# Gate and up products by seven block products for eight, and the down projection in three parts

## The chip, the cores and the metric

One core of a Trainium2 chip runs the whole program. The metric is the device time of one execution in microseconds (us), lower is better; each kernel's time is the median of several executions. The engines are TensorE (PE, with its weight loads as PEld), VectorE (DVE), ScalarE (ACT), GpSimd (POOL) and SyncE (SP, which here only issues loads).

## The reference

One sequence of 512 tokens and 1024 features passes two layers. Each layer is a feed-forward half step, a token mixer (attention, of two kinds in layer 0 and of one in layer 1) and a second feed-forward half step; each of these has its own norm, and a shift, scale and gate computed from a conditioning vector `c`:

```python
def ffn(u, w_gate, w_up, w_down):          # 1024 -> 2816 -> 1024
    return (silu(u @ w_gate) * (u @ w_up)) @ w_down
mod = c_act @ ada_w[l] + ada_b[l]          # nine vectors: shift, scale, gate of three sub-layers
h = h + 0.5 * gate * ffn(rmsnorm(h) * (1 + scale) + shift, ...)
```

All of it is float32. The four feed-forwards are called here FFN 1 (layer 0, before the mixer), FFN 2 (layer 0, after it), FFN 3 and FFN 4 (layer 1).

## The kernel before, in words

**Layout.** Activations lie transposed: features on the 128 partitions, 512 tokens along the free axis, so an activation of 1024 features is eight tiles of 128x512 (KD = 8). Every float32 operand is held as a rounded high part and a low remainder (`u` pairs, `wh`/`wl`), and a product of two of them is three matmuls in the reduced format (`mm3`, L297 to L301: high by high, high by low, low by high). A weight block of 128x1024 is loaded into `raw` (two buffers), ACT copies it to `wh` (L265), DVE subtracts to get `wl` (L266); `wchunk` is load and split together.

**Feed-forward (`ffn`, L542).** 2816 hidden features are 22 tiles of 128 (NF). For one hidden tile, gate is 8 k-blocks x 3 = 24 matmuls of 512 columns into a PSUM bank `pj`, up 24 more into `s`; `gated` (L553) then makes silu on ACT (L556), the product with up on DVE (L557), and splits the result into a hidden pair (`split`, L349 on ACT and L350 on DVE). GpSimd has no part in it. The first tiles (three in FFN 1, interleaved with the making of the input by `first_feed`; two in the others) are done apart, in the others in two token halves of 256 columns so that they can begin when the first half of the norm is done. After all 22 tiles, `back_proj` (L474) makes down: for each of eight output tiles 22 x 3 matmuls over the hidden pairs, and `Back.tile` (L441) adds the bank times the gate vector to the residual `h`. The last output tile is done in two token halves, each followed by the statistics and the norm for the next sub-layer (`nxt` from `u_next`, L604).

**Modulation.** `ada_chunk` (L183) loads 128x1024 of the modulation weights into one of two `wide` buffers through SP and lets DVE multiply it by the conditioning vector with a running sum (L186); eight chunks make one gate or shift vector. They wait in a list, `pending`, and `background(n)` takes n of them after a hidden tile (3 in FFN 1, 4 in FFN 2, 2 in the others) or a down tile (3). `need` (L255) takes as many as a missing vector asks for.

**Order.** Tiles are written in program order; the framework adds the waits, `tc.issue_after` and `tc.high_priority` move the marked instructions. Each engine then runs its own list in order. The lists of both kernels are known, and places of them stand below.

The changed kernel's own line numbers are used for what only it has.

Of the kernel before, what the change touches and what calls it, by code (L numbers as in the profile page):

```python
# [16 lines left out]
P = 128  # L17
NT = 5
NRAW = 2
# [18 lines left out]
T = 512  # L38
# [58 lines left out]
def kernel(ctx: ExitStack, tc: tile.TileContext, d):  # L97
# [84 lines left out]

    def ada_chunk(l, j, k, raw=None):  # L183
# [227 lines left out]
    def affine(src, rb, k, a, b, oh, ol):  # L411
        t = t_tile()[:, :src.shape[-1]]
# [129 lines left out]
    def ffn(l, f, u, gate, nxt, feed=None, rate=2, after=None):  # L542
# [22 lines left out]

        if feed is not None:
# [22 lines left out]
        for j in range(j0, NF):  # L589
            unit(j, *load(j), 0, T)  # L590
            background(rate)
            if after is not None and j == after[0]:
                after[1]()

        def down(k):
            out = []
            for c, (k0, k1) in enumerate(((0, 8), (8, 16), (16, 22))):
                wh, wl = wchunk(d["wd"][l, f, k][:, k0 * P:k1 * P], (k1 - k0) * P)
                out.append((wh, wl, k1 - k0))
            return out  # L600

        back_proj(gate(), down, hidden, nxt, 1)

    def u_next(l, sub):  # L604
        outs = [(u_tile(), u_tile()) for _ in range(KD)]

        def nxt(acc, c0, c1):
# [619 lines left out]
    turned = []  # L1227
# [8 lines left out]
    def first_feed(k):  # L1236
# [16 lines left out]
    pending.extend(ada_work(0, [("g", 0), ("n", 1), ("g", 1), ("n", 2), ("g", 2)]))  # L1253
# [13 lines left out]

    for l in range(2):
        n_u, n_nxt = u_next(l, 1)
        ffn(l, 0, u, need(gcol, (l, 0)), n_nxt, first_feed if l == 0 else None, 3,  # L1270
            (NF - 1 if l == 0 else 6, lambda: tables(l)))
        u = n_u
        n_u, n_nxt = u_next(l, 2)
        (hybrid if l == 0 else mla)(u, tabs[l], need(gcol, (l, 1)), n_nxt)
        u = n_u
        if l == 0:
            get_cond()
            pending.extend(ada_work(1, [("n", 0), ("g", 0), ("n", 1), ("g", 1), ("n", 2), ("g", 2)]))
            n_u, n_nxt = u_next(1, 0)
            ffn(0, 1, u, need(gcol, (0, 2)), n_nxt, rate=4)  # L1280
            u = n_u
        else:
# [10 lines left out]
            ffn(1, 1, u, need(gcol, (1, 2)), final)  # L1293
# [24 lines left out]
def _layout(inp):  # L1318
# [18 lines left out]
    out["wgu"] = gu.reshape(2, 2, 2, KD, P, NF, P).transpose(0, 1, 5, 2, 4, 3, 6).reshape(2, 2, NF, 2, P, D)  # L1337
    out["wd"] = a["ffn_w_down"].reshape(2, 2, NF, P, KD, P).transpose(0, 1, 4, 3, 2, 5).reshape(2, 2, KD, P, NF * P)
# [51 lines left out]
```

## Time and profile before

| | |
|---|---|
| median of three runs | 2010.2 us (2007.99 to 2011.35) |
| the profiled execution | 2006.17 us, span 2004.4 us |
| PE busy | 1956.1 us, 98% of the span |
| DVE, ACT, POOL busy | 1094.6, 744.7, 120.4 us |
| POOL busy before 100, 100 to 700, 700 to 1100 us | 0.42, 120.00, 0.00 us |
| mean granted TensorE clock | 0.995 of full speed |

The span runs from the first to the last instruction. Busy time is not the time an engine was needed: an engine can be busy beside another that sets the end. The granted clock is the share of full speed at which TensorE was allowed to run.

### The profile page before, as it was taken

How to read it: one execution, taken by the hardware profiler on the slowest of the kernel's cores; microseconds unless marked ns; L12 is line 12 of the kernel's file. 1: busy time of each engine (PE TensorE's matmuls, PEld its weight loads, DVE VectorE, ACT ScalarE, POOL GpSimd, SP SyncE). 2: the span in 40 equal slices, each digit the busy share in tenths (PEclk: the TensorE clock that was granted, in tenths of full speed). 3: DMA queues.
4: the chain of work that ended last, by engine and by line, in shares of the span. 5: the costliest groups of instructions: out<-in, count | busy, mean ns of one | idle time of the engine just before them, and what ended most of it. 6: DMA issues, size and time to landing. Idle time of an engine off the chain costs nothing.

```text
span 2004.4 us, 25366 instructions
## 1 busy us (share of the span) xinstructions
PE 1956.1 (98%) x9988; PEld 1652.8 (82%) x9988; DVE 1094.6 (55%) x1893; ACT 744.7 (37%) x1232; POOL 120.4 (6%) x116
## 2 busy tenths in 40 slices
PE   7999999999989999999999999999999999999997
PEld 4888888987878888888889888888988898888886
DVE  7466673479946577777336433323586573333234
ACT  6322222246667442222224233222357543232221
POOL 0000000045553000000000000000000000000000
PEclk9999999999999999999999999999999999999998
DMA  9467773232222238887432333233232023322331
GB/s 334 135 228 241 236 234 105 92 107 67 85 79 80 85 121 270 280 274 248 117 97 85 107 99 95 92 98 97 71 99 71 23 94 109 103 95 95 95 97 61
DMA packets 78412, 260.53 MB, mean 130 GB/s; under 512 B 9426, under 2 KB 12498, under 8 KB 78292
## 3 DMA queue, kind: packets, MB, share of 16 engines
q1 hardware_dynamic: 75892, 254.65, 39.5%
q0 software_dynamic: 1664, 3.28, 0.7%
q8 instruction: 78, 1.28, 0.3%
q10 hardware_dynamic: 736, 0.98, 0.2%
q14 instruction: 42, 0.34, 0.1%
HBM read 249.17 MB, written 2.10 MB: 125 GB/s over the span
## 4 chain that ended last, share of the span: by engine, by line
PE 83%; DVE 10%; ACT 3%; DMA 2%; issue 1%; POOL 1%; SPq 0%; DVEq 0%; ACTq 0%; POOLq 0%
PE pj L299 18%; PE pj L301 18%; PE pj L300 18%; PE s L301 9%; PE s L300 9%; PE s L299 9%; DVE hid L978 1%; DVE m L977 1%; DVE wl L266 1%; DVE hid L767 1%; DVE hid L350 1%; DVE sm L699 1%; PE aux L718 1%; ACT wide L707 1%; ACT wh L265 1%
## 5 line engine op out<-in xcount | busy, mean ns | idle before, releaser
L265 ACT ACTIVATE wh<-raw 128x1024 fp32r<-128x1024 f32 (+1 forms) x331 | 340.8, 1030 | 899.6 <-PE pj L300 561.9
L266 DVE TENSOR_TENSOR wl<-raw,wh 128x1024 fp32r<-128x1024 f32 (+2 forms) x308 | 364.6, 1184 | 417.5 <-ACT wh L265 417.0
L299 PE MATMUL pj<-u,wh 128*128 128x512 f32 (+1 forms) x1035 | 391.1, 379 | 2.0 <-ACT u L349 0.9
L301 PE MATMUL pj<-u,wl 128*128 128x512 f32 (+1 forms) x1035 | 382.5, 370 | 0.7 <-DVE wl L266 0.5
L300 PE MATMUL pj<-u,wh 128*128 128x512 f32 (+1 forms) x1035 | 381.4, 370 | 0.8 <-DVE u L350 0.8
L299 PE MATMUL pj<-hid,wh 128*128 128x512 f32 (+1 forms) x876 | 319.5, 365 | 0.2 <-DVE h L441 0.2
L300 PE MATMUL pj<-hid,wh 128*128 128x512 f32 (+1 forms) x876 | 317.2, 362 | 0.0
L301 PE MATMUL pj<-hid,wl 128*128 128x512 f32 (+1 forms) x876 | 317.2, 362 | 0.0
L301 PE MATMUL s<-u,wl 128*128 128x512 f32 (+1 forms) x841 | 311.3, 370 | 0.0
L300 PE MATMUL s<-u,wh 128*128 128x512 f32 (+1 forms) x841 | 310.8, 370 | 0.0
L299 PE MATMUL s<-u,wh 128*128 128x512 f32 (+1 forms) x841 | 310.6, 370 | 0.0
L299 PEld LDWEIGHTS pj<-u,wh 128*128 128x128 f32 x1035 | 196.3, 190 | 35.6 <-issue 3.1
L301 PEld LDWEIGHTS pj<-u,wl 128*128 128x128 f32 x1035 | 195.5, 189 | 34.4 <-DVE wl L266 1.5
L300 PEld LDWEIGHTS pj<-u,wh 128*128 128x128 f32 x1035 | 195.6, 189 | 31.2 <-DVE u L350 1.9
L186 DVE SCALAR_TENSOR_TENSOR wide<-wide,cond 128x1024 f32<-128x1024 f32 x133 | 161.3, 1223 | 73.4 <-DMA wide<-in_ada 73.2
L299 PEld LDWEIGHTS pj<-hid,wh 128*128 128x128 f32 x876 | 165.5, 189 | 25.8 <-DVE hid L770 0.4
L301 PEld LDWEIGHTS pj<-hid,wl 128*128 128x128 f32 x876 | 165.3, 189 | 25.4
L300 PEld LDWEIGHTS pj<-hid,wh 128*128 128x128 f32 x876 | 165.4, 189 | 24.9
L301 PEld LDWEIGHTS s<-u,wl 128*128 128x128 f32 x841 | 158.8, 189 | 26.8
L300 PEld LDWEIGHTS s<-u,wh 128*128 128x128 f32 x841 | 158.6, 189 | 26.5
L299 PEld LDWEIGHTS s<-u,wh 128*128 128x128 f32 x841 | 158.5, 189 | 26.0
L557 DVE TENSOR_TENSOR t<-t,s 128x512 f32<-128x512 f32 (+1 forms) x93 | 60.5, 651 | 162.8 <-PE s L301 159.5
(214 smaller groups left out, 1920.2 us busy)
## 6 DMA issues: line engine op xcount, KB each, us to landing
raw<-in_wgu SPq DMA_DIRECT2D x176, 512.0 KB, 3.5
wide<-in_ada SPq DMA_DIRECT2D x133, 512.0 KB, 4.4
raw<-in_wd SPq DMA_DIRECT2D x64, 512.0 KB, 3.5
raw<-in_wd SPq DMA_DIRECT2D x32, 384.0 KB, 3.1
raw<-in_hin SPq DMA_DIRECT2D x19, 512.0 KB, 3.5
h<-in_ada SPq DMA_DIRECT2D x11, 512.0 KB, 7.1
raw<-in_hv SPq DMA_DIRECT2D x8, 512.0 KB, 3.5
raw<-in_hout SPq DMA_DIRECT2D x8, 512.0 KB, 3.6
```

The costliest lines, as they stand in the source:

```text
L186: V.scalar_tensor_tensor(raw, raw, 1.0, cond[0], op0=ALU.mult, op1=ALU.mult, accum_out=mod[l][:, j, k:k + 1])
L265: S.activation(wh[:, :n], raw[:, :n], AF.Copy)
L266: (by or V).tensor_tensor(wl[:, :n], raw[:, :n], wh[:, :n].bitcast(F32), op=ALU.subtract)
L299: PE.matmul(ps, ah, bh, start=start, stop=False)
L300: PE.matmul(ps, ah, bl, start=False, stop=False)
L301: last_mm[0] = PE.matmul(ps, al, bh, start=False, stop=stop).ins
L350: return V.tensor_tensor(ol, raw, oh.bitcast(F32), op=ALU.subtract)
L557: V.tensor_tensor(sg[:, :w], sg[:, :w], pu[:, :w], op=ALU.mult)
L699: V.tensor_reduce(nmx, ps[:, :n], axis=AX.X, op=ALU.max, negate=True)
L707: S.activation(pr[qt], pr[qt], AF.Copy, scale=rinv[:, qt:qt + 1])
L718: last_mm[0] = PE.transpose(ps[:, c:c + P], pr[qt][:, kt * P:(kt + 1) * P], ident).ins
L767: V.tensor_tensor(ol, ps, oh.bitcast(F32), op=ALU.subtract)
```

## The change

Hidden tiles are taken in pairs (`pair`). For a pair, gate (and then up) is a product of a 256x1024 weight with the 1024x512 input. Weights are cut in blocks a11, a12, a21, a22 (hidden tile of the pair x half of the depth), the input in depth halves and token halves, and the Strassen-Winograd form is used: seven block products of 4 k-blocks x 3 = 12 matmuls of 256 columns each, so 84 matmuls of 256 columns for a form of a pair, where two old tiles take 48 of 512. It needs sums of weight blocks before (`weight_sums`: four GpSimd instructions of 128x512, L577 to L580, then four splits), sums of input blocks once for a feed-forward (`input_sums`, L559 to L562, four GpSimd instructions for each of four k-blocks, and before them, in FFN 2 to 4, eight GpSimd bias additions L735, then 8 splits), and sums of the products behind (DVE L616, L620, L624 from PSUM; GpSimd L621 of 128x256; ACT copies). The silu is made by ACT in place (L656), the product of gate and up by GpSimd (L659, twice), and four quarter splits make the two hidden pairs. There are 39 such pairs: tiles 0 to 3 of FFN 1 and tiles 0 and 1 of the others stay as they were.

Down is made in three parts, over hidden tiles 0 to 5, 6 to 13 and 14 to 21, each after its pairs. The first two add into `h` (L707), the last goes through `back_proj`, now with its last three output tiles in halves. With that the gate vector is asked for after the first part and not after all tiles. `background` takes 1 chunk after a pair and 2 after a down tile; the gate of FFN 2 is moved to after the mixer. `raw` has four buffers for two. The weights come in a second arrangement, `wgs`, built outside the timed program.

```diff
-NRAW = 2
+NRAW = 4
...
+    def input_sums(t1, t2):
+        lo, hi = slice(0, HALF), slice(HALF, T)
+        G.tensor_tensor(t1[:, lo], t1[:, hi], t1[:, lo], op=ALU.subtract)
+        G.tensor_tensor(t1[:, hi], t1[:, hi], t2[:, hi], op=ALU.add)
+        G.tensor_tensor(t2[:, hi], t2[:, hi], t1[:, lo], op=ALU.add)
+        G.tensor_tensor(t2[:, lo], t2[:, lo], t2[:, hi], op=ALU.subtract)
...
+    def weight_sums(ap):
+        r = [raw_tile() for _ in range(3)]
+        a21, a22 = hid_tile(F32), hid_tile(F32)
+        for i, o in enumerate((r[0][:, :T], r[0][:, T:], a21, a22)):
+            nc.sync.dma_start(o, ap[i])
+        (a11, a12), (s2, s1), (s3, s4) = [(x[:, :T], x[:, T:]) for x in r]
+        G.tensor_tensor(s3, a21, a11, op=ALU.subtract)
+        G.tensor_tensor(s2, a22, s3, op=ALU.subtract)
+        G.tensor_tensor(s1, a21, a22, op=ALU.subtract)
+        G.tensor_tensor(s4, a12, s2, op=ALU.subtract)
+        w = [wsplit(x, n) for x, n in ((r[0], 2 * T), (r[1], 2 * T), (r[2], 2 * T), (a22, T))]
...
+        product(b1[:, lo], "A11", block(0, lo))
+        S.activation(t[:, lo], b1[:, lo], AF.Copy)
+        product(b26[:, lo], "A12", block(1, lo))
+        product(b26[:, hi], "S2", lambda q: sums[q][1])
+        V.tensor_tensor(two(ca), twice(t[:, lo]), two(b26), op=ALU.add)
+        product(b57[:, lo], "S1", lambda q: sums[q][0])
+        product(b57[:, hi], "S3", lambda q: sums[q][2])
+        S.activation(t[:, hi], b57[:, lo], AF.Copy)
+        V.tensor_tensor(two(cb), twice(ca[:, hi]), two(b57), op=ALU.add)
+        G.tensor_tensor(ca[:, hi], cb[:, hi], t[:, hi], op=ALU.add)
+        product(b34[:, lo], "S4", block(1, hi))
+        product(b34[:, hi], "A22", lambda q: sums[q][3])
+        V.tensor_tensor(cb, cb, b34, op=ALU.add)
+        return ca, cb
...
+        def pair(j):
+            g = pair_products(d["wgs"][l, f, j // 2, 0], u, sums)
+            for x in g:
+                S.activation(x, x, AF.Silu)
+            p = pair_products(d["wgs"][l, f, j // 2, 1], u, sums)
+            for x, y in zip(p, g):
+                G.tensor_tensor(x, x, y, op=ALU.mult)
...
-        for j in range(j0, NF):
-            unit(j, *load(j), 0, T)
-            background(rate)
...
-        back_proj(gate(), down, hidden, nxt, 1)
...
+        for p0, p1 in PARTS:
+            for j in range(max(j0, p0), p1, 2):
+                pair(j)
+            if after is not None and p1 == NF:
+                after()
+            act = hidden[p0:p1]
...
+            g = gate()
+            if p1 < NF:
+                for k in range(KD):
+                    ps = pj_ps()
+                    run_tile(ps, down(k), act, 0, T)
+                    mark[0] = V.scalar_tensor_tensor(h[:, k], ps, g[:, k:k + 1], h[:, k],
+                                                     op0=ALU.mult, op1=ALU.add).ins
+                    background(rate[1])
+            else:
+                back_proj(g, down, act, nxt, 3)
...
+                        for k in (2 * q, 2 * q + 1):
+                            G.tensor_scalar(kept[k], kept[k], bcol[l, sub][:, k:k + 1], None, op0=ALU.add)
+                        sums.append(input_sums(kept[2 * q], kept[2 * q + 1]))
```

Three places of the new lists. In them a name is followed by its numbers.

GpSimd, from the end of one pair of FFN 1 into the next (`hid_288`, `hid_289` hold up, `hid_268`, `hid_269` gate, `raw_296` a11 and a12 of the next pair's gate, `hid_299` and `hid_300` its a21 and a22):

```order
45 L621 TENSOR_TENSOR hid_288_1393<-hid_289_1394,t_290_1395 128x256
46 L659 TENSOR_TENSOR hid_288_1393<-hid_288_1393,hid_268_1265 128x512
47 L659 TENSOR_TENSOR hid_289_1394<-hid_289_1394,hid_269_1266 128x512
48 L577 TENSOR_TENSOR raw_298_1505<-hid_299_1506,raw_296_1503 128x512
49 L578 TENSOR_TENSOR raw_297_1504<-hid_300_1507,raw_298_1505 128x512
50 L579 TENSOR_TENSOR raw_297_1504<-hid_299_1506,hid_300_1507 128x512
51 L580 TENSOR_TENSOR raw_298_1505<-raw_296_1503,raw_297_1504 128x512
52 L621 TENSOR_TENSOR hid_313_1536<-hid_314_1537,t_315_1538 128x256
53 L577 TENSOR_TENSOR raw_318_1633<-hid_319_1634,raw_316_1631 128x512
```

The next pair's sums stand behind the two multiplications of this pair, and the sums of its up behind L621 of its gate; before, GpSimd had nothing in a feed-forward.

TensorE, gate of the same next pair, from the end of its A12 product (`wh_301` holds a11 and a12, `wh_303` S2 and S1, `wh_305` S3 and S4):

```order
728 L302 MATMUL s_310_1533<-u_24_128,wh_301_1516 128x256
729 L303 MATMUL s_310_1533<-u_25_129,wh_301_1516 128x256
730 L304 MATMUL s_310_1533<-u_24_128,wl_302_1517 128x256
731 L302 MATMUL s_310_1533<-hid_92_291,wh_303_1520 128x256
732 L303 MATMUL s_310_1533<-hid_93_292,wh_303_1520 128x256
733 L302 MATMUL aux_311_1534<-hid_90_287,wh_303_1520 128x256
734 L303 MATMUL aux_311_1534<-hid_91_288,wh_303_1520 128x256
735 L302 MATMUL s_312_1535<-u_12_116,wh_305_1524 128x256
736 L304 MATMUL s_310_1533<-hid_92_291,wl_304_1521 128x256
737 L302 MATMUL s_310_1533<-hid_111_392,wh_303_1520 128x256
```

Ahead of row 728 stand the other 23 matmuls of A11 and A12, which need no sum; behind row 735 stand 55 more of this form. Before, all 24 matmuls of a gate tile needed one load and one split:

```order
239 L299 MATMUL pj_141_635<-u_18_122,wh_136_625 128x512
240 L300 MATMUL pj_141_635<-u_19_123,wh_136_625 128x512
241 L301 MATMUL pj_141_635<-u_18_122,wl_137_626 128x512
242 L299 MATMUL pj_141_635<-u_20_124,wh_136_625 128x512
243 L300 MATMUL pj_141_635<-u_21_125,wh_136_625 128x512
```

What moved: row 735, which reads the fourth of the pair's sums, now stands ahead of nearly all work of the form that the first sums would release.

DVE, the first part of down in FFN 1 (`g_0_0` is its gate vector, L189 the modulation chunk, `wide` its buffers):

```order
113 L269 TENSOR_TENSOR wl_230_1103<-raw_228_1100,wh_229_1102 128x768
114 L189 SCALAR_TENSOR_TENSOR wide_197_950,mod0_92<-wide_197_950,cond_1_94 128x1024
115 L269 TENSOR_TENSOR wl_236_1135<-raw_234_1132,wh_235_1134 128x768
116 L189 SCALAR_TENSOR_TENSOR wide_198_953,mod0_92<-wide_198_953,cond_1_94 128x1024
117 L189 SCALAR_TENSOR_TENSOR wide_199_956,mod0_92<-wide_199_956,cond_1_94 128x1024
118 L189 SCALAR_TENSOR_TENSOR wide_200_959,mod0_92<-wide_200_959,cond_1_94 128x1024
119 L189 SCALAR_TENSOR_TENSOR wide_201_962,mod0_92<-wide_201_962,cond_1_94 128x1024
120 L189 SCALAR_TENSOR_TENSOR wide_202_965,mod0_92<-wide_202_965,cond_1_94 128x1024
121 L211 TENSOR_TENSOR g_0_0_968<-mod0_92,vec_81 128x8
122 L213 TENSOR_SCALAR g_0_0_968<-g_0_0_968 128x8
123 L707 SCALAR_TENSOR_TENSOR h_88<-pj_203_971,g_0_0_968,h_88 128x512
```

Eight chunks in all (two more stand just ahead, rows 111 and 112) are needed for the vector, and the first update of `h` waits for it. Before, the vector was ready at row 114 of DVE's list, and its first user, L441, stood at row 229.

## Rows read from the trace of the kernel before

**Rows 1.** the page, part 1: busy us, share of the span, instructions.
```profile
PE 1956.1 (98%) x9988; PEld 1652.8 (82%) x9988; DVE 1094.6 (55%) x1893; ACT 744.7 (37%) x1232; POOL 120.4 (6%) x116
```

**Rows 2.** the page, part 4: the chain that ended last, by engine.
```profile
PE 83%; DVE 10%; ACT 3%; DMA 2%; issue 1%; POOL 1%; SPq 0%; DVEq 0%; ACTq 0%; POOLq 0%
```

**Rows 3.** stages view, gate and up of the third feed-forward, 50 us.
```profile
1200.00:1250.00 50.00, 50.00 (x223) 41.39 (x222) 17.47 (x19) 14.20 (x18) 0.00 (x0) 1.00 0.32 99
```

**Rows 4.** timeline of PE, first feed-forward: first, last of 54 512-column matmuls.
```profile
99.78 0.39 PE L299 MATMUL s<-u,wh 128*128 128x512 f32 x1
...
111.79 0.39 PE L301 MATMUL s<-u,wl 128*128 128x512 f32 x1
```

**Rows 5.** timeline of PE, hybrid input: first, last of 55 256-column matmuls.
```profile
400.90 0.28 PE L299 MATMUL pj<-u,wh 128*128 128x256 f32 x1
...
407.38 0.28 PE L299 MATMUL pj<-u,wh 128*128 128x256 f32 x1
```

**Rows 6.** groups by shape, POOL: count, busy us, mean ns, idle before.
```profile
L266 POOL TENSOR_TENSOR wl<-raw,wh 128x1024 fp32r<-128x1024 f32 x23 | 56.0, 2439 | 96.7 <-ACT wh L265 90.3 <-PE aux L718 6.4
L658 POOL TENSOR_TENSOR hid<-hid,hid 128x512 f32<-128x512 f32 x8 | 10.3, 1283 | 0.6
L848 POOL MEMSET hid<- 64x512 f32 x8 | 4.1, 519 | 381.4 <-PE pj L301 381.0
```

**Rows 7.** groups by shape, DVE.
```profile
L266 DVE TENSOR_TENSOR wl<-raw,wh 128x1024 fp32r<-128x1024 f32 x268 | 328.0, 1224 | 306.9 <-ACT wh L265 306.4
L186 DVE SCALAR_TENSOR_TENSOR wide<-wide,cond 128x1024 f32<-128x1024 f32 x133 | 161.3, 1223 | 73.4 <-DMA wide<-in_ada 73.2
L557 DVE TENSOR_TENSOR t<-t,s 128x512 f32<-128x512 f32 x81 | 55.5, 686 | 159.5 <-PE s L301 159.5
L350 DVE TENSOR_TENSOR hid<-t,hid 128x256 fp32r<-128x256 f32 x12 | 5.0, 419 | 0.2
```

**Rows 8.** groups by shape, ACT.
```profile
L265 ACT ACTIVATE wh<-raw 128x1024 fp32r<-128x1024 f32 x291 | 308.3, 1059 | 769.5 <-PE pj L300 440.6 <-issue 195.1 <-PE s L300 60.6
L349 ACT ACTIVATE hid<-t 128x256 fp32r<-128x256 f32 x12 | 4.9, 412 | 6.1 <-DVE t L557 6.1
```

**Rows 9.** timeline of POOL, hybrid mixer: start, us, line, operation.
```profile
606.29 1.29 POOL L656 TENSOR_TENSOR hid<-hid,rope 128x512 f32<-128x512 f32 x1 [0.79 <-DMA hid<-hid]
607.54 1.74 POOL L657 TENSOR_TENSOR hid<-hid,rope 128x512 f32<-128x512 f32 x1
```

**Rows 10.** timeline of DVE at the same moment (two instructions, merged).
```profile
605.65 2.47 DVE L767 TENSOR_TENSOR hid<-hid,hid 64x512 fp32r<-64x512 f32 x2
```

**Rows 11.** timeline of PE: the longest idle spans of the mixer, in brackets.
```profile
426.71 0.39 PE L300 MATMUL pj<-wl,u 128*128 128x256 f32 x1 [2.62 <-POOL wl L266]
590.70 0.55 PE L294 MATMUL s<-hid,hid 128*128 128x256 f32 x1 [5.46 <-DMA hid<-hid]
```

**Rows 12.** stages view, 1 us each, around the idle span that ends at 590.70.
```profile
587.00:588.00 1.00, 0.00 (x0) 0.00 (x0) 0.00 (x0) 0.61 (x1) 0.36 (x1) 0.74 0.00 0
588.00:589.00 1.00, 0.00 (x0) 0.00 (x0) 0.92 (x2) 0.95 (x3) 0.59 (x2) 0.50 0.00 0
...
594.00:595.00 1.00, 1.00 (x5) 0.65 (x4) 0.00 (x0) 0.00 (x0) 0.63 (x1) 0.84 0.28 86
595.00:596.00 1.00, 1.00 (x6) 0.81 (x5) 0.69 (x1) 0.20 (x1) 1.00 (x2) 1.00 0.88 324
```

**Rows 13.** the page, part 6: modulation weight loads, KB each, us to landing.
```profile
wide<-in_ada SPq DMA_DIRECT2D x133, 512.0 KB, 4.4
```

**Rows 14.** timeline of DVE, second half of the norm before the second feed-forward.
```profile
714.32 0.48 DVE L413 SCALAR_TENSOR_TENSOR t<-h,a,aux 128x256 f32<-128x256 f32 x1 [0.28 <-PE aux L403]
...
720.17 0.47 DVE L418 SCALAR_TENSOR_TENSOR u<-t,b,u 128x256 fp32r<-128x256 f32 x1
```

**Rows 15.** timeline of PE: last 256-column matmul of the first two tiles there.
```profile
728.50 0.28 PE L301 MATMUL s<-u,wl 128*128 128x256 f32 x1
```

**Rows 16.** stages view, 10 us of the first stage.
```profile
20.00:30.00 10.00, 8.31 (x27) 5.88 (x26) 9.78 (x19) 7.40 (x12) 0.00 (x0) 1.00 0.85 295
```

More of the change, by code (lines that the diff above doesn't have):

```diff
@@ L181, with raw_tile @@
     mark = [None]
+    def raw_tile():
+        return wp.tile([P, 1024], F32, tag="raw", name=nm("raw"), bufs=NRAW)
     def ada_chunk(l, j, k, raw=None):
@@ L540, in first_products @@
             mm3(ps, wh[:, sl], wl[:, sl], *u[k], k == 0, k == KD - 1)
-    def ffn(l, f, u, gate, nxt, feed=None, rate=2, after=None):
+    HALF = T // 2
+    def input_sums(t1, t2):
[4 more added lines that the diff above has]
+        G.tensor_tensor(t2[:, lo], t2[:, lo], t2[:, hi], op=ALU.subtract)
+        out = []
+        for t in (t1, t2):
+            o = hid_tile(), hid_tile()
+            split(*o, t)
+            out += [tuple(x[:, c] for x in o) for c in (lo, hi)]
+        return [out[0], out[3], out[1], out[2]]
@@ new lines, with pair_products, product, block @@
+    banks = [0]
+    def pair_products(ap, u, sums):
+        w = weight_sums(ap)
+        banks[0] += 1
+        b1, b26, b57, b34 = pj_ps(), s_ps(), aux_ps(), s_ps() if banks[0] % 2 else aux_ps()
+        lo, hi = slice(0, HALF), slice(HALF, T)
+        def product(o, name, b):
+            wh, wl = w[name]
+            for q in range(KD // 2):
+                sl = slice(q * P, (q + 1) * P)
+                mm3(o, wh[:, sl], wl[:, sl], *b(q), q == 0, q == KD // 2 - 1)
+        def block(i, c):
+            return lambda q: [y[:, c] for y in u[2 * q + i]]
+        def two(x):
+            return x.rearrange("p (s c) -> p s c", s=2)
+        def twice(x):
+            return x.unsqueeze(1).to_broadcast([P, 2, HALF])
+        ca, cb, t = hid_tile(F32), hid_tile(F32), t_tile()
+        product(b1[:, lo], "A11", block(0, lo))
[12 more added lines that the diff above has]
+        return ca, cb
@@ L543, in ffn @@
+    PARTS = ((0, 6), (6, 14), (14, 22))
+    def ffn(l, f, u, sums, gate, nxt, feed=None, rate=(2, 2), after=None):
         hidden = []
@@ L588, in ffn, with down, u_next @@
                     gated(j, *pss, c0, c1)
-        for j in range(j0, NF):
-            unit(j, *load(j), 0, T)
-            background(rate)
[L592 to L600, printed above, removed]
-        back_proj(gate(), down, hidden, nxt, 1)
-    def u_next(l, sub):
+        for p0, p1 in PARTS:
[4 more added lines that the diff above has]
+            act = hidden[p0:p1]
+            def down(k):
+                return [(*wchunk(d["wd"][l, f, k][:, p0 * P:p1 * P], (p1 - p0) * P), p1 - p0)]
+            g = gate()
[8 more added lines that the diff above has]
+                back_proj(g, down, act, nxt, 3)
+    def u_next(l, sub, keep=False):
         outs = [(u_tile(), u_tile()) for _ in range(KD)]
+        kept, sums = [], []
         def nxt(acc, c0, c1):
```

69 lines of the change are left out of this document (47 added, 22 removed).

## The prediction

> **What bounds the kernel now.** I read the page's busy times first: TensorE is busy for 98% of the span, DVE for 55%, ACT for 37% and GpSimd for 6% [rows 1]. The chain that ended last is 83% TensorE [rows 2]. In a stretch of gate and up TensorE has no gap at all in 50 us, and DVE and ACT are busy for 17.47 and 14.20 us of it [rows 3]: there a matmul saved is time saved, and a wait put ahead of a matmul is time added, since there is no slack to take it. The timelines give the price of a matmul. From the first to the last of 54 matmuls of 512 columns 12.01 us pass, 0.2266 us each [rows 4]; from the first to the last of 55 of 256 columns 6.48 us, 0.120 us each [rows 5].
>
> **The change part by part.** The sum goes by the profiled execution, 2006.2 us; the median of the runs is 4 us higher, which I add at the end.
>
> *Fewer columns.* A form of a pair took 48 x 0.2266 = 10.88 us and now takes 84 x 0.120 = 10.08 us [rows 4, 5]. Seven eighths of the columns are left, but a matmul of half the width costs more than half. The gain is 0.80 us a form, 1.6 a pair, 39 x 1.6 = 62 us for the kernel, if everything else is hidden: an old pair is 21.76 us, a new one 20.16.
>
> The Trainium skill (TensorE: Matmul & The Clock Gate, section Back-to-back issue gap) gives N/2.4 + 2.5 ns as the gap of single matmuls at the full clock. By it a form would fall from 10.36 to 9.17 us and the kernel gain 93 us; rows 4 and 5 are longer than that at both widths, so I keep to the rows.
>
> *A pair in the middle of a part: the wait for the sums.* The order fixes the chain. GpSimd makes the next pair's weight sums only after both multiplications L659 of this pair, and the second of these needs L624, which needs the last product of up. Call its end 0. On TensorE 24 matmuls follow that need no sum: they last until 24 x 0.120 = 2.88. Meanwhile: L624 follows a split that waits for ACT and ends at 1.9 (0.69 of it its own, by the like instruction L557 [rows 7]; the rest an ACT copy and a DVE split of 0.41 and 0.42 [rows 7, 8] and passing on). Multiplication at 2.2 to 3.5, sums of 1.28 us each (L658, the same shape [rows 6]).
>
> Whether DVE and GpSimd can work at once matters here. In the mixer GpSimd's instruction at 606.29 ran for its normal 1.29 us, while two DVE instructions on half the partitions, with two SBUF operands, took 2.47 us together; then the next one of GpSimd took 1.74 [rows 9, 10]. So one waits for the other. The Trainium skill (SBUF — State Buffer, section Who interferes with whom) says the same as a rule: a DVE instruction with two SBUF inputs and a GpSimd instruction exclude each other. The trace agrees, and the rule speaks against this change, which puts 14.2 us of GpSimd work (ten instructions of 1.28 us, two of 0.71) beside DVE splits in every pair.
>
> So the two remaining splits (2 x 0.42 [rows 7]) push the sums. The third ends near 8.0 and the ACT copy of its weights (1.06 [rows 8]) at 9.06; the fourth at 9.3, its copy at 10.4. With a modulation chunk's 1.22 us (L186 [rows 7]) between, 11.6. TensorE thus idles from 2.88 to about 9, and its row 735 holds the rest until 10.4. Then 55 matmuls, 6.6 us.
>
> An idle span of this length costs twice. After 5.46 us without work [rows 11] the granted clock fell from full speed to 0.50, the lower of the two levels (1.2 GHz), and it returned only in the slice after 594 [rows 12]: some 3.6 us of work at half speed, 1.8 us lost. After an idle span of 2.62 us [rows 11] no such fall showed. The new one is 6.2 us, nearer to the first; I take 1.8 us, bounds 0 and 1.8. Gate of the pair ends at 18.8.
>
> Up: its sums stand behind L621 of gate, which follows the S3 product (2.6 us before gate's end) by 0.17 + 0.69 + 0.71 (the last an estimate, from 1.28 for 512 columns [rows 6]). Four sums and the ACT copy end at 24.0, while TensorE has work until 18.8 + 2.88 = 21.7; 54 matmuls are left, 6.5 us, with small waits 30.7. That is +8.9 against 21.76, and +10.1 with a chunk. By the order 27 of the 39 pairs stand behind another pair, 13 of them with a chunk: 14 x 8.9 + 13 x 10.1 = **+256 us**. Without the fall of the clock and any exclusion a pair would be 28.1 us, 27 x 6.3 = +170: the lower bound.
>
> *First pairs of a part.* In the second and third parts eight pairs come after down tiles, whose 18 or 24 matmuls of 512 columns a tile cover the sums; I take 21.6, nothing gained for want of time for up's sums. The other four first pairs stand in the next term.
>
> *Start of FFN 2 to 4.* The norm's second half makes the input on DVE from 714.32 to 720.17 [rows 14], and the first two tiles last until 728.50 [rows 15]. Now GpSimd must add the bias to eight tiles and make 16 sums: 8 x (0.52 to 1.28) + 16 x 0.71 = 15.5 to 21.6 us (L848 and L658 [rows 6] as bounds of the addition), plus waits for DVE, then three weight sums (3.8) and two splits (2.4). TensorE's cover is the first tiles' second half, 11.5 us, and 2.88. Stall 10 to 19, I take 14, three times 42, and 2 us each at half clock: **+48 us**.
>
> *The gate vector asked for early.* In FFN 1 and FFN 2 the first update of `h` waits for eight (seven) chunks; two PSUM banks let TensorE go on for two tiles, 2 x 18 x 0.2266 = 8.2 us. A chunk lands 4.4 us after its issue [rows 13] and is then used for 1.22 us; with two buffers, (4.4 + 1.3) / 2 = 2.85 each, 8 x 2.85 = 23, so 15 us of stall in each. Behind it on SP's queue stand 22 loads of chunks ahead of the next pair's a21 and a22; I take 10 us more each. With 4 for the clock: **+53 us**; bounds 20 and 100.
>
> *First stage of FFN 1.* DVE is busy there for 9.78 of 10 us [rows 16], and gets eight more splits of 0.69: **+5**.
>
> *Rest.* First pairs -1. The three parts add 16 updates of `h` in each feed-forward, beside matmuls; more `raw` buffers and three halved output tiles show no price here: 0, within 5 either way.
>
> Sum: 2006.2 + 256 + 48 + 53 + 5 - 1 = 2367, and 4 for the median: **2371 us**.
>
> **The rivals.**
> - *DVE and GpSimd do not exclude each other in these forms.* For it: the new sums read fp32 operands in other places. Against: rows 9 and 10. A mid pair is 29.9, 27 x 8.1 = 219, starts at 40: about 2326.
> - *Short waits.* The clock stays up and the starts and vectors cost their lower bounds: 2010 + 170 + 30 + 20 = 2230. Against: rows 11 and 12.
> - *The other side: the sums come ahead.* If weight sums and their copies were done by the time the 24 free matmuls end, every pair would be 20.16 us: 2010 - 62 + 5 = about 1953, faster. The place is GpSimd's list between L659 and L577; it decides at 2.88 - 1.06 = 1.8 us after the last product, and by my chain the multiplication before the sums begins at 2.2. Against it is the order itself; for it only that I may have misread what the multiplication waits for.
> - *TensorE stays at half clock through the mid pairs.* The idle spans recur every 31 us. Some 85 matmuls more at half speed would add 10 us a pair, 27 x 10 = 270: about 2640. Against: the clock returned within 4 us at 594 [rows 12].
> - *Chunks come one at a time.* If buffers let a load start only after the use before it, and the weights queue behind all 22, each chunk costs 5.7 us and the third term doubles: about 2425.
> - *The change does not do what it says*: excluded by the new list, which has 84 matmuls of 256 columns a form.
>
> **How the numbers follow.** A measurement of this kernel tells 0.2%, about 4 us, from no change. Chances: my forecast 0.60, no exclusion 0.17, short waits 0.06, the other side 0.04, clock down 0.05, chunks one at a time 0.08. The range of 2230 to 2470 leaves out the other side and the clock, about 0.1, and a little of the forecast's own error (each mid pair missed by 3 us moves the sum by 81). Faster 0.04, the same 0.01, slower 0.95.
>
> **What would show it.** In the new profile: GpSimd busy for over 700 us (39 x 14.2, the input sums, and the 120 of before) and TensorE for 80 to 85% of the span; in mid pairs an idle span of TensorE of 5 to 7 us that a split of S2 (behind GpSimd) ends, a shorter one in up, a pair every 30 to 32 us; a granted clock below full speed behind the long spans; splits of DVE longer than their own time beside GpSimd; three stalls of 10 to 19 us after the first tiles of FFN 2 to 4; two at the first down part of FFN 1 and FFN 2, ended by DVE's updates L707. I am wrong if pairs take 22 us or less, or if the time of the stalls sits at loads of `wgs`.

## The result and the profile after

The changed kernel takes 2464.8 us (median of 4 runs, 2462.3 to 2470.1) where the kernel before takes 2009.1 beside it: ratio 1.2273, 95% interval 1.2244 to 1.2302. It is slower by 456 us. The prediction was 2371 us in a range of 2230 to 2470: the direction and the mechanism came true, the size was 94 us short, and the time lies only 5 us under the upper end of the range.

The page of the changed kernel, busy times and the chain that ended last:

```profile
PE 2062.9 (84%) x12813; PEld 1858.7 (75%) x12820; DVE 1525.3 (62%) x2395; ACT 962.7 (39%) x1662; POOL 822.1 (33%) x672
...
PE 18%; issue 16%; POOL 16%; DVE 5%; DMA 4%; ACT 3%; POOLq 0%; DVEq 0%; SPq 0%; ACTq 0%
```

Against [rows 1, 2] TensorE falls from 98% to 84% of the span; GpSimd, 120 us before, is busy for 822 us. The shares of the chain add up to 62% of the span, since it is followed back only to 931 us; in that part GpSimd has 16% and TensorE 18%, where before TensorE had 83% of a whole chain. Summed over 1-us slices, TensorE's idle time grows from 48 to 402 us, and busy time weighted with what the clock lacked from 4 to 142 us. Together that is 492 us; 31 of the 62 us of saved columns are left against it; where the other 31 went no run shows.

A stretch of gate and up in feed-forward 3, in the view of [rows 3]; and TensorE there, the idle time before a row in brackets:

```profile
1540.00:1590.00 50.00, 40.05 (x292) 38.44 (x293) 26.40 (x30) 20.74 (x31) 20.54 (x18) 0.89 0.25 80
```

```profile
1540.37 0.58 PE L302 MATMUL s<-hid,wh 128*128 128x256 f32 x1 [5.93 <-ACT wh L268]
...
1553.85 0.39 PE L302 MATMUL s<-hid,wh 128*128 128x256 f32 x1 [1.32 <-ACT wh L268]
1555.08 0.39 PE L302 MATMUL aux<-u,wh 128*128 128x256 f32 x1 [0.48 <-ACT wh L268]
...
1570.89 0.58 PE L302 MATMUL s<-hid,wh 128*128 128x256 f32 x1 [5.95 <-ACT wh L268]
```

This repeats in every middle pair: gate's S2 weights come 5.9 us late, up's 1.3 us. GpSimd in the same stretch, timeline, from the multiplication that the pair's last product releases:

```profile
1564.33 1.39 POOL L659 TENSOR_TENSOR hid<-hid,hid 128x512 f32<-128x512 f32 x1 [1.58 <-DVE hid L624]
1565.68 1.26 POOL L577 TENSOR_TENSOR raw<-hid,raw 128x512 f32<-128x512 f32 x1
1567.02 1.32 POOL L578 TENSOR_TENSOR raw<-hid,raw 128x512 f32<-128x512 f32 x1
1568.31 1.44 POOL L579 TENSOR_TENSOR raw<-hid,hid 128x512 f32<-128x512 f32 x1
1569.71 1.26 POOL L580 TENSOR_TENSOR raw<-raw,raw 128x512 f32<-128x512 f32 x1
```

The chain is the one of the prediction: VectorE's L624, multiplication, three sums, ACT's copy (1.06 us), then TensorE at 1570.89. From one pair's L624 to the next 30.5 us pass (1533.06 to 1563.58). In feed-forward 1, with a modulation chunk, it is 34.0 us (222.50 to 256.47). GpSimd's fourth sum and VectorE's chunk there:

```profile
261.20 1.44 POOL L579 TENSOR_TENSOR raw<-hid,hid 128x512 f32<-128x512 f32 x1
262.61 2.25 POOL L580 TENSOR_TENSOR raw<-raw,raw 128x512 f32<-128x512 f32 x1
```

```profile
261.44 2.28 DVE L189 SCALAR_TENSOR_TENSOR wide<-wide,cond 128x1024 f32<-128x1024 f32 x1
```

Alone such instructions take 1.28 [rows 6] and 1.22 us [rows 7]; side by side 2.25 and 2.28. The chunk, first in place at 261.44, ends 1.1 us after L579 has ended, and L580 1.1 us after the chunk, which fits each waiting until the other has done. And the clock (its column is third from the right), in the gate form without a chunk, then in an up form behind idle spans of only 1.33 and 0.49 us:

```profile
1543.00:1544.00 1.00, 1.00 (x7) 1.00 (x6) 1.00 (x2) 0.01 (x1) 0.00 (x0) 0.50 0.16 18
1544.00:1545.00 1.00, 1.00 (x10) 1.00 (x10) 1.00 (x2) 0.00 (x0) 0.00 (x0) 0.97 0.94 287
...
246.00:247.00 1.00, 0.51 (x5) 0.51 (x5) 1.00 (x2) 1.00 (x3) 0.00 (x0) 0.99 0.00 0
247.00:248.00 1.00, 1.00 (x7) 1.00 (x7) 1.00 (x2) 0.91 (x1) 0.00 (x0) 0.50 0.00 0
```

So the clock falls once in each of the 13 middle pairs without a chunk and twice in each of the 14 with one, the second time behind spans that I had held harmless. The same two spans did no harm in feed-forward 3 (1.32 and 0.48 us at 1553.85 and 1555.08, clock 1.00 throughout).

### The profile page after: what moved, and what is told of

It is laid out like the page before. It is cut to its first block, busy times and chain, and to the rows that moved or that the text cites. A ratio compares the mean times of both kernels' runs of the same rounds, so it can differ in the third digit from the quotient of the medians.

```text
span 2465.5 us, 33493 instructions
## 1 busy us (share of the span) xinstructions
PE 2062.9 (84%) x12813; PEld 1858.7 (75%) x12820; DVE 1525.3 (62%) x2395; ACT 962.7 (39%) x1662; POOL 822.1 (33%) x672
## 3 DMA queue, kind: packets, MB, share of 16 engines
q1 hardware_dynamic: 98356, 254.66, 30.7%
## 4 chain that ended last, share of the span: by engine, by line
PE 18%; issue 16%; POOL 16%; DVE 5%; DMA 4%; ACT 3%; POOLq 0%; DVEq 0%; SPq 0%; ACTq 0%
DMA wide<-in_ada 3%; POOL raw L580 3%; PE pj L303 3%; POOL raw L579 3%; PE pj L302 3%; PE pj L304 3%; POOL raw L578 3%; POOL raw L577 3%; POOL hid L659 2%; PE aux L302 2%; ACT wh L268 2%; DVE wide L189 1%; PE s L304 1%; PE aux L304 1%; PE aux L303 1%
## 5 line engine op out<-in xcount | busy, mean ns | idle before, releaser
L268 ACT ACTIVATE wh<-raw 128x1024 fp32r<-128x1024 f32 (+2 forms) x409 | 421.7, 1032 | 587.2 <-PE pj L303 303.4
L269 DVE TENSOR_TENSOR wl<-raw,wh 128x1024 fp32r<-128x1024 f32 (+2 forms) x386 | 482.5, 1251 | 246.8 <-ACT wh L268 243.6
L302 PE MATMUL s<-hid,wh 128*128 128x256 f32 (+1 forms) x488 | 175.1, 359 | 248.2 <-ACT wh L268 248.2
L621 POOL TENSOR_TENSOR hid<-hid,t 128x256 f32<-128x256 f32 x78 | 58.6, 751 | 761.5 <-DVE hid L620 713.4
L302 PE MATMUL pj<-u,wh 128*128 128x256 f32 (+1 forms) x723 | 241.1, 334 | 21.7 <-ACT wh L268 9.1
L353 DVE TENSOR_TENSOR hid<-hid,hid 128x256 fp32r<-128x256 f32 (+2 forms) x192 | 143.2, 766 | 164.3 <-ACT hid L352 163.8
L302 PE MATMUL aux<-hid,wh 128*128 128x256 f32 x780 | 238.1, 305 | 0.0
L304 PE MATMUL aux<-hid,wl 128*128 128x256 f32 x780 | 236.1, 303 | 0.0
L303 PE MATMUL aux<-hid,wh 128*128 128x256 f32 x780 | 235.9, 302 | 0.0
L303 PE MATMUL pj<-u,wh 128*128 128x256 f32 (+1 forms) x723 | 232.0, 321 | 3.9 <-DVE u L353 2.5
L304 PE MATMUL pj<-u,wl 128*128 128x256 f32 (+1 forms) x723 | 231.4, 320 | 2.2 <-DVE wl L269 2.2
L302 PE MATMUL s<-u,wh 128*128 128x256 f32 (+1 forms) x685 | 211.6, 309 | 14.6 <-ACT wh L268 14.6
L302 PEld LDWEIGHTS pj<-hid,wh 128*128 128x128 f32 x884 | 169.1, 191 | 63.2 <-DVE h L707 29.5
L189 DVE SCALAR_TENSOR_TENSOR wide<-wide,cond 128x1024 f32<-128x1024 f32 x133 | 185.2, 1395 | 48.9 <-DMA wide<-in_ada 48.4
L303 PE MATMUL s<-u,wh 128*128 128x256 f32 (+1 forms) x685 | 202.6, 296 | 0.0
L304 PE MATMUL s<-u,wl 128*128 128x256 f32 (+1 forms) x685 | 201.4, 294 | 0.0
```

Source lines behind the costliest of these rows:

```text
L268: S.activation(wh[:, :n], raw[:, :n], AF.Copy)
L269: (by or V).tensor_tensor(wl[:, :n], raw[:, :n], wh[:, :n].bitcast(F32), op=ALU.subtract)
L302: PE.matmul(ps, ah, bh, start=start, stop=False)
L303: PE.matmul(ps, ah, bl, start=False, stop=False)
L304: last_mm[0] = PE.matmul(ps, al, bh, start=False, stop=stop).ins
L353: return V.tensor_tensor(ol, raw, oh.bitcast(F32), op=ALU.subtract)
```

## The experiments

Two theories of the middle pairs: **A**, the order (the sums stand behind multiplications that need the pair's last product); **B**, GpSimd's pace and its exclusion with VectorE. All runs are drawn from the changed kernel unless said otherwise; line numbers are each run's own. The times of c3, c4 and c5 are medians of 12, 5 and 6 executions, the others single executions; the kernel before, executed 17 times beside c3 and c4, took 2005 to 2015 us, so a few us of a single execution tell nothing.

**e1_sums_first**: the next gate's sums ahead of the multiplications.

```diff
+            if more:
+                made.append(weight_sums(d["wgs"][l, f, j // 2 + 1, 0]))
             for x, y in zip(p, g):
-                G.tensor_tensor(x, x, y, op=ALU.mult)
+                with tc.issue_after(made[0][2]) if more else nullcontext():
+                    G.tensor_tensor(x, x, y, op=ALU.mult)
```

> Only GpSimd's order differs from the changed kernel: the next pair's four weight sums stand ahead of the two multiplications of this pair. Theory A (the sums wait in GpSimd's list behind multiplications that need the pair's last product): the gate form gets as short as the up form is (about 12.5 us for 18), the 5.95 us idle spans of TensorE shrink to 1 to 2.5 us, and the clock does not fall there; 27 pairs times about 6.5 us less, so about 2290 us (2260 to 2320). Theory B (GpSimd's speed and its exclusion with VectorE set a pair's length, whatever the order): the wait moves but stays, pairs of 28 us or more, 2360 us or above.

Measured 2379.5 us, 85 less: by the time theory B (2360 or above). TensorE in a pair of feed-forward 4, first the up form's wait, then the next gate's:

```profile
2128.14 0.39 PE L302 MATMUL s<-hid,wh 128*128 128x256 f32 x1 [2.47 <-ACT wh L268]
...
2140.66 0.39 PE L302 MATMUL s<-hid,wh 128*128 128x256 f32 x1 [1.45 <-ACT wh L268]
2141.92 0.39 PE L304 MATMUL s<-hid,wl 128*128 128x256 f32 x1 [0.52 <-DVE wl L269]
...
2145.75 0.39 PE L304 MATMUL aux<-hid,wl 128*128 128x256 f32 x1 [0.78 <-DVE wl L269]
```

Gate's long wait shrinks to 1.45 us as A says, and in that pair the clock stays up; the pair is 27.3 us (L627 at 2123.19 and 2150.49). But up's wait has grown from 1.3 to 2.47 us, and new waits for VectorE's splits appear while GpSimd multiplies. Pairs without a chunk take 27.3 to 29.5 us; in those with one up waits for 3.4 to 4.5 us, the clock falls in all of them, and they take 30.3 to 31.4. So A is right for the gate form, and B has a share.

**e2_mult_ca_dve**: nothing on GpSimd but the sums.

```diff
-                G.tensor_tensor(x, x, y, op=ALU.mult)
+                V.tensor_tensor(x, x, y, op=ALU.mult)
...
-        G.tensor_tensor(ca[:, hi], cb[:, hi], t[:, hi], op=ALU.add)
+        V.tensor_tensor(ca[:, hi], cb[:, hi], t[:, hi], op=ALU.add)
```

> The two multiplications and the 256-column sum of products go from GpSimd to VectorE; GpSimd keeps the weight sums alone, which then need no product. Theory A: the sums run ahead during the form before, no idle span of TensorE over 2 us in a middle pair, a pair of 21 to 23.5 us, about 2200 us (2150 to 2260). Theory B (exclusion): GpSimd's 10.3 us of sums and VectorE's 12.6 us of work with two SBUF operands do not fit beside each other in a pair of 20.2 us, so pairs of 24 us or more and 2260 us or above, with sums and splits drawn out in the trace.

Measured 2264.8 us, at B's edge. GpSimd and VectorE in a pair of feed-forward 4:

```profile
2171.05 2.16 POOL L578 TENSOR_TENSOR raw<-hid,raw 128x512 f32<-128x512 f32 x1 [4.35 <-DVE wl L269]
2173.18 1.74 POOL L579 TENSOR_TENSOR raw<-hid,hid 128x512 f32<-128x512 f32 x1
2174.88 2.27 POOL L580 TENSOR_TENSOR raw<-raw,raw 128x512 f32<-128x512 f32 x1
```

```profile
2169.70 2.36 DVE L269 TENSOR_TENSOR wl<-raw,wh 128x1024 fp32r<-128x1024 f32 x2 [1.91 <-ACT wh L268]
2171.98 1.79 DVE L269 TENSOR_TENSOR wl<-hid,wh 128x512 fp32r<-128x512 f32 x1
```

The sums no longer need a product, and now they are drawn out to 1.7 to 2.3 us, and VectorE's split of 0.68 to 1.79. Pairs are 23 to 25 us, with a chunk 27.5 in the mean. The first line shows a third wait, which neither theory has: L578 waits for 4.35 us until VectorE's split has freed the `raw` buffer that it writes. What it costs is not told apart here.

**e3_no_weight_sums**, with the same loads and splits:

```diff
-        G.tensor_tensor(s3, a21, a11, op=ALU.subtract)
...
-        w = [wsplit(x, n) for x, n in ((r[0], 2 * T), (r[1], 2 * T), (r[2], 2 * T), (a22, T))]
+        w = [wsplit(x, n) for x, n in ((r[0], 2 * T), (r[1], 2 * T), (r[0], 2 * T), (r[1], T))]
```

> The four weight sums of a form are left out: S1 to S4 are replaced by blocks as loaded (the products are then not those of the reference), with as many loads, copies and splits. What stays is everything else of the change. Theory A and B alike: middle pairs of about 20.5 to 21.5 us, and the starts of the second to fourth feed-forward (about 16 us each) and the gate vector waits (about 20 us each) remain, so about 2085 us (2050 to 2120). If something other than the weight sums holds the pairs up, above 2150 us.

Measured 2063.6 us, as both expected. Middle pairs take 20.1 us (L618 at 906.98 and 927.07; 20.2 is the mean of the 27, with a chunk or without): TensorE's gain is real, and with the weight sums goes all that holds a middle pair up.

**e4_plain_parts**: the pairs made the old way, the rest of the change kept.

```diff
-            g = pair_products(d["wgs"][l, f, j // 2, 0], u, sums)
...
+            unit(j, *load(j), 0, T)
+            unit(j + 1, *load(j + 1), 0, T)
```

> The pairs are made the old way (two hidden tiles with 512-column matmuls, no sums of any kind), and all the rest of the change stays: down in three parts, the gate vector asked for early, four raw buffers. My step says two waits for the gate vector of about 20 us each with what is queued behind them: about 2055 us (2035 to 2080). Rival (the waits are hidden when loads of the pairs do not queue behind chunks, and parts cost nothing): 2015 us or less. Rival (three parts themselves cost, by 16 more updates of h and more halves): 2090 us or above.

Measured 2060.2 us where the kernel before took 2006.9. The two waits stand where they were said to be:

```profile
118.48 0.80 PE L302 MATMUL pj<-hid,wh 128*128 128x512 f32 x1 [14.61 <-DVE h L698]
...
821.19 0.80 PE L302 MATMUL pj<-hid,wh 128*128 128x512 f32 x1 [13.15 <-DVE h L698]
```

By VectorE's updates of `h`, FFN 1 is 19 us longer than before and FFN 2 20 us; 7 us each fall to the mixer and to FFN 3; FFN 4, with its down in three parts, is as long as before. There the parts themselves cost nothing; the 7 us of FFN 3 stand at its start, where TensorE idles for 2.97 and 1.11 us in the norm (1117.09, 1119.39) and works at half clock until 1123.7.

**e5_warm**: 40 idle-time matmuls in gate forms.

```diff
         product(b26[:, lo], "A12", block(1, lo))
+        for _ in range(warm):
+            PE.matmul(b26[:, hi], w["A11"][0][:, :P], u[0][0][:, lo], start=True, stop=True)
```

> The changed kernel with 40 more matmuls of 256 columns (4.8 us at full speed) in the gate form of the 27 middle pairs, behind the A12 product; they write into a bank half that the S2 product overwrites, and read what is there. They do nothing but keep TensorE at work in the idle span of 5.95 us. Theory (the idle spans cost a second time, by the lower clock behind them): the clock stays up, no time is added since the sums come no sooner, and most of the some 100 us of half clock in middle pairs comes back: about 2385 us (2350 to 2410), mean clock 0.95 or more. Rival (the wait chain alone sets a pair's length, and the slower matmuls behind it are hidden under the next chain): 2450 us or above.

Measured 2440.2 us, mean clock 0.952: the clock as the theory says, the time short of the rival's 2450 and far from the theory's 2385. Three whole pairs, two of FFN 2 with a chunk and one of FFN 4 without:

```profile
1027.26:1058.06 30.80, 25.99 (x210) 25.16 (x209) 18.70 (x21) 11.42 (x18) 15.43 (x12) 1.00 0.25 86
1191.67:1225.29 33.62, 28.96 (x210) 28.14 (x209) 18.93 (x21) 11.41 (x18) 15.43 (x12) 0.90 0.24 79
2156.71:2187.86 31.15, 27.48 (x210) 26.66 (x209) 15.58 (x19) 11.30 (x18) 14.43 (x12) 0.95 0.21 68
```

Of the 14 pairs with a chunk seven lose both falls and take 29.8 to 30.8 us; in the second part of FFN 2 that is some 3 us less than in the changed kernel (30.8 for 33.8). One keeps one fall, and six keep two, with idle spans of 1.3 to 1.7 us as in the others, these taking 33.5 to 33.8. Of the 13 without a chunk eleven keep one fall, now in the up form, and take 29.8 to 31.2 us, no less than before; the two without any take 29.7. So two falls are worth some 3 us in a pair with a chunk, one in a pair without less than 1 us. Which idle span makes the clock fall is not told by its length alone. Why it held in one place and not in the other stays open.

**e6_all_dve**: as e2, and the four weight sums on VectorE (`G` to `V` in L577 to L580).

> Multiplications, the 256-column sums and the weight sums all go from GpSimd to VectorE, whose work rises to 22.1 us a pair; GpSimd keeps only the input sums. The weight sums stand again behind the multiplications and splits, now in VectorE's list. Theory B (exclusion of the two engines kept the second run's pairs at 24 to 27 us): without it, though VectorE has 5.4 us more a pair, pairs of 23.5 to 25.5 us and about 2180 us (2140 to 2215). Rival (exclusion matters little, VectorE's work and the order do): not faster than the second run, 2265 us or above.

Measured 2312.4 us: the rival was right. Without any exclusion, but with the sums again behind multiplications and splits, TensorE waits in a pair of FFN 4 as follows, the clock falls behind it, and the pair is 27.3 us:

```profile
2230.03 0.39 PE L302 MATMUL s<-hid,wh 128*128 128x256 f32 x1 [3.22 <-ACT wh L268]
...
2243.15 0.39 PE L302 MATMUL s<-hid,wh 128*128 128x256 f32 x1 [0.86 <-ACT wh L268]
```

Curing the order alone (e2) brings 200 us, curing the exclusion alone (this run) 152, and pairs without a chunk are left at 23 to 27 us. That order costs more than exclusion is likely but not shown: e2 also takes work off GpSimd, and this run puts more on VectorE.

**e7_no_sums**: as e3, and the products read input blocks instead of input sums, which are not made; of the lines beside those of e3:

```diff
+        sums = [[[y[:, c] for y in u[2 * q + i]] for i in (0, 1) for c in (slice(0, HALF), slice(HALF, T))] for q in range(KD // 2)]
...
-            first_sums.append(input_sums(*first_t[-2:]))
```

> As the third run, without weight sums, and without the input sums too: the input blocks take their place (the products are not those of the reference). The difference from the third run is the price of input sums at the starts and in the first stage. My step gave 48 us for the three starts and 5 for the first stage: about 2015 us (2000 to 2030). Rival (the starts stall for the first splits after the norm anyway): 2045 us or above.

Measured 2022.5 us, as expected: the input sums cost 41 us without weight sums beside them.

**c1_mixed**, the first attempt at a faster version; its core:

```diff
+                if isinstance(j, int):
+                    pair(j, then)
+                else:
+                    w = load(j[0])
+                    then()
+                    unit(j[0], *w, 0, T)
```

`then` makes the next form's weight sums, now on VectorE, ahead of this tile's products.

> A version drawn from the runs so far. Feed-forwards 1 and 2 are made with plain tiles, down in two parts (tiles 0 to 13, 14 to 21), so that the gate vector is ready long ahead. In feed-forwards 3 and 4 every second pair, ten in all, is made with seven products; its sums, multiplications and splits stand on VectorE, the weight sums one form ahead, so that a plain pair's slack on VectorE carries them. If the wait is the order and the engines' exclusion and nothing else, these pairs take 20.2 to 21 us for 21.76: about 1996 us (1988 to 2006). Rival (starts with input sums, or VectorE's list, eat the 16 us): 2008 us or above.

Measured 2016.7 us for 2009.4: the rival. The ten pairs have no gap, but FFN 3 and FFN 4 are no shorter (366.4 and 364.6 us for 364.5 and 364.8), since their starts give it back in idle spans and half clock (FFN 4: 3.06 and 1.43 us idle, half clock from 1654.2 to 1661.0), and the mixer of layer 0 is 7 us longer. GpSimd makes input sums within the norm there, and ACT's split of one stands in its list ahead of the norm's own L420:

```profile
1648.66 3.57 POOL L759 TENSOR_SCALAR hid<-hid,b 128x512 f32<-128x512 f32 x2 [530.13 <-DVE u L421]
1652.20 0.72 POOL L559 TENSOR_TENSOR hid<-hid 128x256 f32<-128x256 f32 x1
1653.00 0.72 POOL L560 TENSOR_TENSOR hid<-hid,hid 128x256 f32<-128x256 f32 x1
```

```profile
1653.76 0.63 ACT L352 ACTIVATE hid<-hid 128x512 fp32r<-128x512 f32 x1 [3.58 <-POOL hid L560]
```

```profile
1654.84 0.58 PE L302 MATMUL pj<-u,wh 128*128 128x256 f32 x1 [3.06 <-ACT u L420]
```

The changed kernel has the same span of 3.06 us at its FFN 4.

**e8_before_raw4**, drawn from the kernel before:

```diff
-NRAW = 2
+NRAW = 4
...
```

> The kernel before, with the change's four raw buffers for two (and its smaller scratch for descriptors, which makes the room), nothing else. In the changed kernel and in every run drawn from it so far the hybrid mixer took some 6 us longer than before, though the change does not touch it; there GpSimd's weight splits run back to back and one VectorE split beside them takes 8.14 us. Theory C (more raw buffers let GpSimd's splits come closer together, and VectorE gets no turn between them): the mixer is 5 to 8 us longer, about 2015 us (2012 to 2018). Rival (something else of the change does it): the time of the kernel before, within 2 us.

Measured 2008.2 us, no difference in time that a single execution could tell. The mechanism is there, at half its size: GpSimd's splits run back to back from 416.88, two DVE instructions (417.46, 419.77) take 2.38 and 5.33 us beside them, TensorE's wait at 433.81 is 6.62 us (before, 2.62 there [rows 11] and 0.85 three us ahead), and the mixer is 3 us longer. The other 3 us stay open.

**c3_mixed and c4_mixed**: two `raw` buffers and two more for the sums alone; FFN 1 as before; input sums on VectorE behind the norm; eight, and twelve, pairs of seven products. The line in which the two runs differ:

```diff
-                work += [j] if l and j in (8, 12, 16, 20) else [(j,), (j + 1,)]
+                work += [j] if l and j in (8, 10, 12, 16, 18, 20) else [(j,), (j + 1,)]
```

> As the eighth run, mended where its trace shows time lost: two raw buffers as before and two more that only the sums use, feed-forward 1 exactly as before, the input sums on VectorE and after the norm instead of on GpSimd within it, and four pairs of seven products in each of feed-forwards 3 and 4 (tiles 8, 12, 16, 20). Eight pairs at 1.6 us less each, no idle span added: about 1997 us where the kernel before takes 2009, ratio 0.994 (0.991 to 0.998). Rival (the clock or VectorE's list takes it back at the starts): ratio 1.000 or above.

> As the run before, with six pairs of seven products in feed-forwards 3 and 4 (tiles 8, 10, 12, 16, 18, 20), so that two or three stand one behind the other. VectorE then has 22.1 us of work in pairs of 20.2 us of TensorE, carried only by the plain pairs between. Theory: throughput of VectorE holds over three pairs, twelve pairs at 1.2 to 1.6 us less: ratio 0.992 (0.989 to 0.996), better than the run before. Rival (a pair behind a pair waits for VectorE by 2 us or more): no better than the run before.

c3: 2001.2 us, ratio 0.9961 (0.9949 to 0.9973). c4: **1990.5 us, ratio 0.9914 (0.9900 to 0.9927)**, faster than both kernels. FFN 3 and FFN 4 take 354.9 and 355.3 us for 364.5 and 364.8: 9.5 us each from six pairs, 1.6 a pair, the whole of what the rows promised. Sixty us of c4 with three such pairs in a row:

```profile
1324.00:1384.00 60.00, 60.00 (x490) 59.43 (x489) 57.63 (x87) 32.09 (x51) 0.00 (x0) 1.00 0.32 102
```

TensorE has no gap, GpSimd nothing to do, and VectorE is busy for 57.63 us of 60: 2.4 us are left, too little for a fourth pair.

**c5_mixed**: six such pairs in FFN 2 as well.

> As the last version, with six pairs of seven products in feed-forward 2 too (its down part then in the three parts of the change, its gate vector still made ready in feed-forward 1), and its modulation chunks only behind plain tiles and down tiles. Theory (gate vector early enough and sums one form ahead: nothing waits): six more pairs at 1.6 us less, ratio 0.987 (0.983 to 0.991). Rival (the chunks, 1.2 us of VectorE each, no longer fit beside the sums, and late ones are waited for): ratio 0.992 or above.

Measured 2000.9 us, ratio 0.9954 (0.9939 to 0.9969), no better than c3: the rival. FFN 2 takes 378.5 us for 367.3 in c4. A stretch of it, and a wait in it:

```profile
830.00:865.00 35.00, 25.68 (x160) 23.57 (x159) 30.21 (x50) 9.87 (x14) 0.00 (x0) 0.85 0.74 245
```

```profile
851.96 1.23 DVE L194 SCALAR_TENSOR_TENSOR wide<-wide,cond 128x1024 f32<-128x1024 f32 x1 [0.72 <-DMA wide<-in_ada]
853.72 0.68 DVE L584 TENSOR_TENSOR rawb<-hid,hid 128x512 f32<-128x512 f32 x1
...
855.61 0.39 PE L307 MATMUL s<-hid,wh 128*128 128x256 f32 x1 [3.53 <-ACT wh L273]
```

Chunks (1.22 us every 2 to 3 us on VectorE there) stand between the sums, VectorE waits for some of their loads, and ACT's copy, which TensorE waits for, waits for the sum L584. That the chunks make up the whole loss is argued from this stretch; no run leaves them out.

## Why the prediction was right, and where its sum was short

Measured are intervals between VectorE's L624, L707 and L445 (L557 and L441 before), against the same work before; middle and first pairs are set against the 21.76 us of the prediction. In FFN 2 two old tiles took 23.1 us, so that some 9 us of the first row belong to the last:

| Term | Predicted, us | Measured, us |
|---|---|---|
| 27 middle pairs | +256 | 14 x 11.9 + 13 x 8.6 = +278 |
| starts of FFN 2 to 4 | +48 | 21 + 27 + 25 = +74 |
| first pairs of parts 2 and 3 | -1 (with the rest) | 8 pairs of 26.1 for 21.76: +35 |
| gate vector, two places | +53 | 21 + 19 = +40 |
| first stage of FFN 1 | +5 | +11 |
| mixers | 0 | +6 |
| the rest, in the down parts | 0 | +18 |

*Fewer columns.* The pairs of 20.1 us in e3 are the 20.16 us of the rows. By the gap that the Trainium skill gives (TensorE: Matmul & The Clock Gate, section Back-to-back issue gap) 168 matmuls would take 18.3 us, an estimate that the run does not bear out.

*A pair in the middle of a part.* Right in place, order and size: pairs without a chunk are 30.3 us (mean of 13) for 30.7 predicted. Pairs with one are 33.6 (mean of 14; I had counted 13) for 31.9: the step "with a modulation chunk's 1.22 us" was mis-sized, since the chunk itself was drawn out to 2.28 us, the half clock behind the long span lasted longer (work from 229.81 to 236.8, where without a chunk it is 1540.37 to 1544.1), and the clock fell a second time.

*An idle span of this length costs twice.* The step took 1.8 us and one fall; e5 shows some 3 us where both falls of a pair with a chunk are gone, and under 1 us for the one fall of a pair without. Its lower reference, no fall behind 2.62 us [rows 11], was a misreading: in the kernel before, too, the clock fell as that span ended at 426.71, and it was back only after 430.

```profile
426.00:427.00 1.00, 0.29 (x2) 0.29 (x3) 1.00 (x1) 0.54 (x2) 0.94 (x2) 1.00 0.00 0
...
428.00:429.00 1.00, 1.00 (x7) 1.00 (x7) 0.97 (x2) 0.98 (x2) 1.00 (x1) 0.50 0.73 246
```

Read rightly, it would have made a fall behind up's wait likely too (24.0 - 21.7 = 2.3 us in my sum); in the changed kernel falls stand behind spans of 1.2 or 1.3 us with one of 0.5 us after it.

*First pairs of a part.* "I take 21.6" failed: up's sums wait behind gate's L621 in these pairs too, the idle spans of 1.22 and 0.49 us are followed by a fall (1653 to 1656), and the eight cost 4.3 us each in the mean, 3.6 the undisturbed ones. This is the largest miss of the sum, 36 us.

*Start of FFN 2 to 4.* The stall of 14 us is about right (15 to 19 us idle); missing are the half clock (4 to 8 us each, I took 2), the late norm (3.06 us, ACT's list), and a bias addition of 1.86 us in the mean, outside the bounds of 0.52 to 1.28.

*The gate vector.* 19 to 21 us each; the 10 us for loads behind chunks did not come in full (6.42 and 6.80 us of idle, part of which any first pair has; they stand in the row of the first pairs).

*Exclusion.* Here the runs corrected me in kind: I priced GpSimd's waits for VectorE, not VectorE's for GpSimd. A split of 128x256 takes 751 ns in the mean in the changed kernel for 419 [rows 7], and e1 and e2 show what that does to TensorE. The Trainium skill (SBUF — State Buffer, section Who interferes with whom) calls the port pair that VectorE and GpSimd share an exclusive lock. L580 and L189, at 2.25 and 2.28 us and each ending its own time after the other, agree; in the mixer a VectorE split even waited through three instructions of GpSimd.

The rival of the other side, sums that come ahead, was rightly placed: it needed another order, and c4 is that order for twelve pairs. Its price of 1953 us was not right, since it left out the sum's own terms for the starts and the gate vector: e3, whose middle pairs take 20.1 us, still measures 2063.6.

That the time lies in the range at all owes something to luck. The terms that I had at nothing, first pairs, mixers and down parts, came to some 59 us, and the low gate vector term gave 13 back; the upper end of 2470 was not drawn with them in mind.

## What to carry to other kernels

Count a saving in matmuls on the engine that gets the extra work, and look in its list for what stands between the producer and the consumer: here a saving of 1.6 us a pair cost 9 to 12, because sums that need no product stood behind a multiplication that does. Make such operands one form ahead, keep them on one of two engines that hold each other up, and use the cheaper form only as often as that engine has slack: twelve pairs gave 0.86%, 39 cost 23%. A short idle span of TensorE can cost more than its own length: half clock may follow it, though e5 shows that this need not show in the time.

## What was not expected of the hardware

- Two more load buffers lengthened a mixer that nobody touched, by 3 us in e8 (in the changed kernel and c1 it is 6 to 7 us longer): GpSimd's three splits ran back to back, and a VectorE split of 64x512, where a like instruction takes 0.68 us alone, took 8.14 us beside them (in c1):

```profile
416.98 8.14 DVE L353 TENSOR_TENSOR hid<-hid,hid 64x512 fp32r<-64x512 f32 x1
```

```profile
416.90 2.41 POOL L269 TENSOR_TENSOR wl<-raw,wh 128x1024 fp32r<-128x1024 f32 x1
...
419.79 4.77 POOL L269 TENSOR_TENSOR wl<-raw,wh 128x1024 fp32r<-128x1024 f32 x2
```

- The clock fell to half behind idle spans of only 1.33 and 0.49 us (FFN 1), and held through spans as long in FFN 3 and in FFN 2 of e5.
- GpSimd's tensor-by-column addition of 128x512 took 1.86 us in the mean of 24 (1.56 at the least), longer than its sum of two tensors (1.28 us [rows 6]).
